# First phase by rows of four column blocks, norm factors by transposes, one small product block later

## The chip, the core and the metric

The kernel runs on one core of a Trainium2 chip. The metric is the device time of one execution in microseconds. The engines are TensorE (PE, matmuls; PEld is its weight load, which overlaps them), VectorE (DVE), ScalarE (ACT), GpSimd (POOL) and SyncE (SP, which issues most transfers).

## The reference

One layer of a hybrid decoder: 528 tokens (16 learned ones and 512 of x), 2048 features. The normalised input goes through one input projection, whose columns feed three causal mixers (gated DeltaNet with 6 heads, GLA with 5, forgetting attention with 5). Each branch has a SiLU gate, and one output projection with a residual and a last norm follows.

```python
h = rms_norm(x, norm_w)                       # x * rsqrt(mean(x*x) + eps) * norm_w
proj = (h @ w_in).astype(f32)                 # [528, 2048] @ [2048, IN_COLS]
(dq, dk, dv, dz, db, da, gq, gk, gv, gz, gl, fq, fk, fv, fz, ff) = split_cols(proj)
...
sol = lax.linalg.triangular_solve(eye + a_mat, rhs, ...)   # DeltaNet, chunks of 64
...
o_dn = gated_head_norm(o_dn, dz, dn_norm_w)
...
return x + o @ w_out                          # then rms_norm(., final_norm_w) over x's tokens
```

## The kernel before

x is held transposed: 16 tiles k of 128 features by 528 tokens. A projection block is 128 columns of `w_in`: its 16 weight tiles (128 x 128, one for each k) are multiplied with the 16 tiles of x and summed in PSUM. For accuracy each operand is split exactly into a high and a low part (`hi`, `lo` of a weight, `xh`, `xl` of x). ACT makes the high part by a cast, DVE the low part by a subtraction, and PE runs three products for each k: hi·xh, hi·xl, lo·xh. x is scaled by `norm_w` (one column of `cpk` for each k) in that split. The factor of each token, 1/rms, is applied later, when a block leaves PSUM: `rstd` holds it for all 128 partitions.

The first phase makes the four blocks `dz` 0 to 3 for the 512 tokens of x, without the learned ones, into four PSUM banks (`pp`). Its weights come by quarters: one transfer holds four k of one block, 128 x 512 numbers (`first_quarter`), so that a quarter of the phase has four transfers, casts and subtractions of weights (`w0q` to `w3q`), and four tiles of x. `load_x` splits x; `first_part` (L303) runs the products. x's tiles 0 and 1 come in a transfer each, the others in pairs. The scales come from `consts` in a transfer of their own that ACT issues (L122). Ten products of the tile `ones` stand ahead of the phase (L298), and one more behind its first matmul group (L324).

While the phase runs, ACT squares the tokens of `xtok` and `mtok` and sums them into `ssq`; `rsc` is 1/rms, one number for each token, tokens along partitions, five columns of 128. To bring it to all partitions, DVE makes five diagonal matrices `dg` (L347) and PE multiplies them with `ones` (L349) into `pr`; ACT copies it to `rstd`. The gate product (`pgate`, L420) is next on PE, then the block `dz` 4 and so on (L234). The gate values run through DVE and ACT into a scan (`gw`, L457), which PE transposes (`ptg`, L462) in the middle of block 4.

The triangular solve is a blockwise inverse (`dn_inverse`, for the heads' groups g = 0 and 1): inverses of 32 x 32 blocks on DVE, then products `pm` (L773) and `pl` (L782), 24 small ones each, with ACT copies between, then `pn` (L808). They are dropped into the row of projection matmuls by `behind(mm, n)`, which ties a product behind the n-th matmul of a projection counted from a mark.

A tile framework orders the instructions of each engine by a simulated timeline, within the ties that the code gives (`behind`, `paced`, priorities); each engine then runs its list in order. Tiles come from pools with a fixed number of buffers, and a transfer into a buffer waits until its former content was read: `raw` rows have 7 buffers, the pool `six` has 14, the token tiles `xt` share 6.

Of the kernel before, what the change touches and what calls it, by code (L numbers as in the profile page):

```python
# [8 lines left out]
F32 = mybir.dt.float32  # L9
F32R = mybir.dt.float32r  # L10
# [3 lines left out]
AF = mybir.ActivationFunctionType  # L14
ALU = mybir.AluOpType
# [3 lines left out]
P = 128  # L19
D = 2048  # L20
KT = D // P
NM = 16
S = 512
T = NM + S
# [7 lines left out]

DN_HEADS, GLA_HEADS, FOX_HEADS = 6, 5, 5
SH = 10
NK = 8
H1 = 1
SKIP = 1
# [40 lines left out]
GATE_COLS, COLS, BLOCK_OF = _cols()  # L78
# [1 line left out]


@with_exitstack
def tile_hybrid_trunk(ctx, tc, xT, xtok, mtok, w_gate, w_in, w_out, w_dn, consts, lmask, fin_w, out, dbg=None):
    nc = tc.nc
    ctx.enter_context(nc.allow_low_precision("operands are split exactly into two parts"))
    dbg = dbg or {}
# [4 lines left out]
    six = pool("six", 14)  # L91
# [8 lines left out]
    def t15(name, shape=(P, H, P), dt=F32):  # L100
        return wk.tile(list(shape), dt, tag="t15", bufs=6, name=name)

    V, A, G, PE = nc.vector, nc.scalar, nc.gpsimd, nc.tensor
# [7 lines left out]
    ident = cst.tile([P, P], F32, name="ident")  # L111
    make_identity(nc, ident)
    ones = t15("ones", (P, P))
# [6 lines left out]
    nwc, cwc = cpk[:, 0:16], cpk[:, 16:88].rearrange("p (b w) -> p b w", w=4)  # L120
# [50 lines left out]
    pace, splits, heads_, waits = [None, None], [], [], []  # L171
# [7 lines left out]
    def raw_rows(src, name):  # L179

        raw = row(f"raw{name}")[:, : src.shape[-1]]
        nc.sync.dma_start(out=raw, in_=src)
        return raw, name

    def split_rows(raw, name):

        n = raw.shape[-1]
        both = six.tile([P, 2, 512], F32R, tag="six", name=f"w{name}")
        hi, lo = both[:, 0, :n], both[:, 1, :n]
        split(raw, hi, lo)  # L190
        return hi, lo


    def part(name, n=512):
        return hp.tile([P, T], F32R, tag="x", name=name)[:, :n]
# [18 lines left out]
    def behind(mm, n):  # L214

        later.append((mm.ins, len(order) + n))
# [9 lines left out]
    xh, xl = [], []  # L226
# [29 lines left out]

    NF = 4

    def first_quarter(i, q):
        return raw_rows(w_in[BLOCK_OF["dz", i], q // 2][:, (q % 2) * 512 : (q % 2 + 1) * 512], f"{i}q{q}")

    xs = {}

    def fetch_x(c):
        xs[c] = six.tile([P, 2, T], F32, tag="six", name=f"xs{c}")
        if c > 0:
            nc.sync.dma_start(out=xs[c], in_=xT[:, 2 * c : 2 * c + 2, :])

    firsts = []

    def fetch_first():
        fetch_x(0)
        for j in range(2):
            nc.sync.dma_start(out=xs[0][:, j], in_=xT[:, j])
            firsts.append(first_quarter(j, 0))
        firsts.extend(first_quarter(i, 0) for i in (2, 3))
        fetch_x(1)

    def load_x(c):
        if c not in xs:
            fetch_x(c)
        t = xs[c]
        for j in range(2):
            k = 2 * c + j
            if c == 0 and j == 1:
                wq.append(split_rows(*firsts[0]))
            xh.append(part(f"xh{k}", T))
            xl.append(part(f"xl{k}", T))  # L290
            A.activation(xh[k], t[:, j], AF.Copy, scale=nwc[:, k : k + 1])
            V.scalar_tensor_tensor(out=xl[k], in0=t[:, j], scalar=nwc[:, k : k + 1],
                                   in1=xh[k].bitcast(F32), op0=ALU.mult, op1=ALU.subtract)


    pw = psm.tile([P, 512], F32, tag="m", name="warm")
    for i in range(10):
        PE.matmul(pw[:, :P], ones, ones, start=True, stop=True)  # L298

    def first_part(ps, q, hi, lo, j):  # L300
        k = 4 * q + j
        for wt, xx in ((hi, xh), (hi, xl), (lo, xh)):
            mm = PE.matmul(ps[:, :S], wt[:, j * P : (j + 1) * P], xx[k][:, NM:T],  # L303
                      start=(k == 0 and wt is hi and xx is xh), stop=(k == KT - 1 and wt is lo))
        return mm

    fetch_first()
    begun = [inproj_begin(("dz", h), False)[1:] for h in range(NF)]
    for q in range(4):
        wq = []  # L310
        load_x(2 * q)
        for i in range(NF):
            if q + i > 0:
                wq.append(split_rows(*(first_quarter(i, q) if q else firsts[i])))
            if i == 1 and q or i == NF - 1 and not q:
                load_x(2 * q + 1)
        for j in range(4):
            for i in range(NF):
                mm = first_part(begun[i][0][0], q, *wq[i], j)
                if q + j + i == 0:  # L320

                    with tc.issue_after(mm.ins):
                        for _ in range(1):
                            PE.matmul(pw[:, :P], ones, ones, start=True, stop=True)  # L324
        if q == 1:
            more_constants()
    for h in range(NF):
        done["dz", h] = [(p_[:, :n], t0, n) for p_, (t0, n) in zip(*begun[h])]
# [2 lines left out]
    rsc = wk.tile([P, 5], F32, tag="rsc", bufs=1, name="rsc")  # L331
# [10 lines left out]
    A.activation(rsc, rsc, AF.Exp, scale=-0.5)  # L342
    pr = [psm.tile([P, 512], F32, tag="m", name=f"pr{a}") for a in range(2)]
    for b in range(5):
        r = NM if b == 4 else P
        dg = t15(f"dg{b}", (P, P))
        V.tensor_scalar_mul(dg[:, :r], ident[:, :r], rsc[:, b : b + 1])  # L347
        o = pr[1][:, :NM] if b == 4 else pr[0][:, b * P : (b + 1) * P]
        PE.matmul(o, ones, dg[:, :r], start=True, stop=True)  # L349
    A.copy(rstd[:, NM:], pr[0])  # L350
    A.copy(rstd[:, :NM], pr[1][:, :NM])

# [275 lines left out]
    raw = {}  # L628
# [99 lines left out]
    def dn_inverse(g, st):  # L728
# [50 lines left out]
        for n in range(NN):  # L779
            for q in range(2):  # L780
                lo_, hi_ = slice(64 * q, 64 * q + 32), slice(64 * q + 32, 64 * q + 64)
                mm = PE.matmul(pl[lo_, n, :], xc[lo_, n, :], m1[lo_, n, :], start=True, stop=True)  # L782
                if g == 1 and n + q == 0:
                    behind(mm, PM[g] + 38)
        for q in range(2):
            A.copy(l1[64 * q : 64 * q + 32], pl[64 * q : 64 * q + 32])

# [843 lines left out]
def _layout(x, meta_tokens, norm_w, w_in, conv_w, a_log, dt_bias, dn_norm_w, w_gk2, b_gk,  # L1631
            gla_norm_w, b_f, w_out, final_norm_w):

    import numpy as np

    c = np.ascontiguousarray
    f = np.float32
    x, w_in, w_out = (np.asarray(a) for a in (x, w_in, w_out))
    xt = np.concatenate([np.asarray(meta_tokens), x[0]], 0).T.reshape(KT, P, T)
    wz = np.concatenate([w_in[0], np.zeros((D, 1), f)], 1)  # L1640
    wg = wz[:, np.asarray(GATE_COLS)].reshape(KT, P, 64).transpose(1, 0, 2).reshape(P, 1024)
    wz = wz[:, np.asarray(COLS)].reshape(2, 8, P, NBLK, P)
# [12 lines left out]
    lm = np.stack([(j // (2 * s) == i // (2 * s)) & (j // s % 2 == 0) & (i // s % 2 == 1)  # L1655
                   for s in (16, 8, 4, 2, 1)] + [j == i], 1).astype(np.int32)
    gk = np.zeros((P, 320), f)
    gk[:16] = gk[16:32] = gk[32:48] = np.asarray(w_gk2)[0]
    misc[:16, 7] = misc[16:32, 6] = misc[32:48, 7] = 1
    misc[16:32, 7] = -1  # L1660
    consts = np.concatenate([
        np.asarray(norm_w)[0].reshape(KT, P).T,
        np.asarray(conv_w)[0].reshape(4, 18, P).transpose(2, 1, 0).reshape(P, 72),
        misc, np.asarray(dn_norm_w)[0][:, None], np.asarray(gla_norm_w)[0][:, None],
        np.concatenate([np.asarray(b_gk)[0], np.zeros(64, f)]).reshape(3, P).T, gk], 1)
    return {
        "xT": c(xt.transpose(1, 0, 2)), "xtok": c(x[0]),
        "mtok": c(np.asarray(meta_tokens)),
        "w_gate": c(wg), "w_in": c(wz.transpose(3, 0, 2, 1, 4).reshape(NBLK, 2, P, 1024)),
        "w_out": c(wo.transpose(3, 0, 2, 1, 4).reshape(4, (16 - SH) // 2, P, 1024)),  # L1670
        "w_dn": c(wd.transpose(2, 0, 1, 3)),
        "consts": c(consts), "lmask": c(lm), "fin_w": c(np.asarray(final_norm_w)),
    }
# [15 lines left out]
```

## Time and profile before

| | |
|---|---|
| median of 3 runs | 974.25 us (973.39 to 974.83) |
| the profiled execution | 973.9 us, span 972.2 us |
| PE busy | 962.6 us, 99% |
| PEld busy | 887.4 us, 91% |
| DVE, ACT, POOL busy | 674.2, 476.7, 222.7 us |
| first phase, L303 | first matmul at 5.29 us, last at 50.71 us |
| small products `pl` of group 0 | 223.64 to 225.1 us |

Times in the profile are microseconds from the start of the span. A row of the timeline gives start, duration, engine, line, operation, output and inputs, the shapes, how many instructions it merges, and in brackets how long the engine was idle before it and what ended that. Matmuls are pipelined, so that their durations overlap; what one costs is the distance from its start to the next one's.

### The profile page before, as it was taken

To read this page: it belongs to the slowest core of one execution; us is meant where nothing else is said; L and a number is where in the kernel's file an instruction comes from. 1 tells how busy PE (TensorE), PEld (TensorE's weight loads), DVE (VectorE), ACT (ScalarE), POOL (GpSimd) and SP (SyncE) were. 2 spreads that over 40 slices of the span, in tenths; PEclk is the share of its full clock that TensorE was granted. 3 is DMA by queue.
4 is the path that set the end of the run, shared out by engine and by line. 5 is a ranking of instruction groups with operands and counts; after the bars stand their busy time and mean duration, and the time that the engine had idled before them with its cause. 6 is when DMAs were issued, how large, how long until landed. Compare 5 with 4: busy or idle time off the path is not lost.

```text
span 972.2 us, 18945 instructions
## 1 busy us (share of the span) xinstructions
PE 962.6 (99%) x7314; PEld 887.4 (91%) x7314; DVE 674.2 (69%) x1468; ACT 476.7 (49%) x1045; POOL 222.7 (23%) x243
## 2 busy tenths in 40 slices
PE   9999999999999999999999999999999999999996
PEld 7899999899999988899999989899999997888885
DVE  5468777877557986434695958866766768986664
ACT  6754533344456233434545545555555545654345
POOL 0033322232123225111213223222332120000023
PEclk9999999999999999999999999999999999999999
DMA  9835577987557797744647575577775588366534
GB/s 341 304 136 208 171 208 214 288 232 212 172 166 209 231 236 189 187 118 104 160 135 188 148 191 180 177 223 211 208 211 158 175 281 280 131 216 212 180 129 174
DMA packets 70335, 191.86 MB, mean 197 GB/s; under 512 B 14077, under 2 KB 17325, under 8 KB 69476
## 3 DMA queue, kind: packets, MB, share of 16 engines
q1 hardware_dynamic: 46048, 152.63, 44.7%
q0 software_dynamic: 15104, 31.66, 18.3%
q10 hardware_dynamic: 9092, 6.36, 2.4%
q8 instruction: 57, 0.93, 0.4%
q14 instruction: 34, 0.28, 0.1%
HBM read 179.93 MB, written 60.88 MB: 248 GB/s over the span
## 4 chain that ended last, share of the span: by engine, by line
PE 98%; DVE 1%; DMA 0%; issue 0%; ACT 0%; SPq 0%; DVEq 0%
PE pp L234 49%; PE pp_a L572 8%; PE pq L1413 6%; PE pp L303 5%; PE pa L1413 3%; PE pt L1413 3%; PE ps L1413 3%; PE pp_c L572 2%; PE pp_d L572 2%; PE pp_b L572 2%; PE pr L1413 1%; PE pss L1058 1%; PE pfo L1288 1%; PE pgate L420 1%; PE pfa L1240 1%; PE pg L716 1%
## 5 line engine op out<-in xcount | busy, mean ns | idle before, releaser
L234 PE MATMUL pp<-xh,wlo 128*128 128x264 f32 (+2 forms) x1120 | 269.8, 306 | 0.0
L234 PE MATMUL pp<-xl,whi 128*128 128x264 f32 (+2 forms) x1120 | 269.8, 305 | 0.0
L234 PE MATMUL pp<-xh,whi 128*128 128x264 f32 (+2 forms) x1120 | 269.7, 306 | 0.0
L166 ACT CAST whi<-raw 128x1024 fp32r<-128x1024 f32 x131 | 137.2, 1047 | 180.0 <-PE pp L234 120.6
L167 DVE TENSOR_TENSOR wlo<-raw,whi 128x1024 fp32r<-128x1024 f32 x131 | 161.0, 1229 | 56.8 <-ACT whi L166 44.4
L234 PEld LDWEIGHTS pp<-xh,whi 128*128 128x128 f32 x1120 | 181.5, 189 | 8.7 <-issue 0.2
L234 PEld LDWEIGHTS pp<-xh,wlo 128*128 128x128 f32 x1120 | 181.6, 189 | 8.5 <-issue 0.2
L234 PEld LDWEIGHTS pp<-xl,whi 128*128 128x128 f32 x1120 | 181.7, 189 | 8.2
L379 POOL TENSOR_SCALAR stc<-cv 128x528 f32<-128x528 f32 (+1 forms) x18 | 27.2, 1513 | 131.3 <-DVE cv L614 120.2
L614 DVE SCALAR_TENSOR_TENSOR cv<-pb,cpk,cv 128x528 f32<-128x528 f32 (+1 forms) x54 | 40.9, 757 | 0.9
L1442 POOL TENSOR_TENSOR acc<-acc,fw 128x512 f32<-128x512 f32 x4 | 6.1, 1544 | 138.7 <-DVE wll L167 138.7
L167 DVE TENSOR_TENSOR wlos<-raws,whis 128x1024 fp32r<-128x1024 f32 x20 | 24.3, 1224 | 14.9 <-ACT whis L166 14.7
L166 ACT CAST whis<-raws 128x1024 fp32r<-128x1024 f32 x20 | 20.7, 1048 | 27.3 <-PE pq L1413 10.3
L572 PE MATMUL pp_a<-t,whi 128*128 128x264 f32 (+1 forms) x224 | 29.5, 282 | 0.0
L572 PE MATMUL pp_a<-xl,whi 128*128 128x264 f32 x112 | 28.4, 288 | 0.0
L572 PE MATMUL pp_a<-xh,whi 128*128 128x264 f32 x112 | 28.1, 285 | 0.0
L486 POOL DMA_DIRECT2D tw<-tw x16 | 13.4, 840 | 62.8 <-DVE wlo L167 30.1
L368 DVE TENSOR_TENSOR pb<-pp,rstd 128x264 f32<-128x264 f32 (+1 forms) x36 | 13.8, 425 | 20.1 <-PE pp L234 20.0
L572 PEld LDWEIGHTS pp_a<-t,whi 128*128 128x128 f32 x224 | 27.7, 189 | 0.0
L379 POOL TENSOR_SCALAR stdz<-zdz 128x512 f32<-128x512 f32 x6 | 11.2, 1874 | 63.7 <-DVE zdz L397 55.3
L1413 PE MATMUL pq<-whia,a 128*128 128x512 f32 x80 | 25.5, 394 | 0.0
L1413 PE MATMUL pq<-whis,s 128*128 128x512 f32 x80 | 25.4, 394 | 0.0
(504 smaller groups left out, 2114.2 us busy)
## 6 DMA issues: line engine op xcount, KB each, us to landing
raw<-in_w_in SPq DMA_DIRECT2D x103, 512.0 KB, 4.0
ti<-in_w_in SPq DMA_DIRECT2D x28, 512.0 KB, 5.2
raw<-ti SPq DMA_DIRECT2D x28, 512.0 KB, 3.4
tw<-in_w_dn SPq DMA_DIRECT2D x20, 512.0 KB, 5.5
raws<-tw SPq DMA_DIRECT2D x15, 512.0 KB, 3.7
ti<-in_w_in POOLq DMA_DIRECT2D x14, 512.0 KB, 7.2
ti<-ti POOLq DMA_DIRECT2D x14, 512.0 KB, 7.5
tw<-in_w_dn POOLq DMA_DIRECT2D x10, 512.0 KB, 6.3
```

The source lines that it names most:

```text
L166: pace[0] = A.copy(hi, raw).ins
L167: pace[1] = V.tensor_tensor(out=lo, in0=raw, in1=hi.bitcast(F32), op=ALU.subtract).ins
L234: mm = PE.matmul(p_[:, :nt], wt[:, j * m : (j + 1) * m], xx[k][:, t0 : t0 + nt], start=(k == 0 and wt is hi and xx is xh), stop=(k == KT - ...
L303: mm = PE.matmul(ps[:, :S], wt[:, j * P : (j + 1) * P], xx[k][:, NM:T], start=(k == 0 and wt is hi and xx is xh), stop=(k == KT - 1 and wt ...
L368: V.tensor_tensor(out=o, in0=p_[rows], in1=rstd[rows, t0 : t0 + n], op=ALU.mult)
L379: maxes.append(G.tensor_scalar_max(t, src, LOW).ins)
L420: PE.matmul(pgate[a][:, :HT], wg[k // 8][:, k % 8, :], xx[k][:, a * HT : (a + 1) * HT], start=(k == 0 and xx is xh), stop=(k == KT - 1 and ...
L486: x = G.dma_start(out=out_[s], in_=in_[s], accum_op=ALU.add, max_dma_last_dim=2048)
L572: m = PE.matmul(p_[:, cols], wt[:, j * P : (j + 1) * P], xx[j][part_][:, cols], start=first and i == 0, stop=i == len(todo) - 1, skip_grou ...
L614: V.scalar_tensor_tensor(out=c, in0=pb[:, t0 + w : w + T], scalar=cwc[:, blk, w : w + 1], in1=c, op0=ALU.mult, op1=ALU.add)
L716: PE.matmul(pg[:r, j * r : (j + 1) * r], kT[:, j, ts], kT[:, j, ts], start=True, stop=True)
L1413: mm = PE.matmul(p_, o_[:, s], w_, start=(first and n == 0), stop=(last and n == 2), skip_group_check=True)
```

## The change

Three things.

The first phase goes by k instead of by quarters. For each k one transfer brings the 128 rows of weights of all four blocks (`w_first`, 128 x 512, laid out for it by the host), one cast and one subtraction split it, and PE runs hi·xh on the four blocks, then hi·xl, then lo·xh. For k = 0 the cast is in two halves of 256 columns. The scales come as 16 further columns of x's first tile (`x_first`) and serve k = 0 and 1; the others use `cpk` as before, whose transfer stays. Transfers are requested two pairs of x tiles ahead. Seven `ones` products stand ahead in place of ten, and the one inside the phase is gone.

The norm factors go to all partitions by five PE transposes of a column of `rsc`, repeated 128 times by its access pattern; the diagonals and their products are gone.

In `dn_inverse` the first product of `pl` of group 0 is tied behind a matmul too (mark `PM[0] + 26`); in group 1 it was already.

```diff
-    def first_quarter(i, q):
-        return raw_rows(w_in[BLOCK_OF["dz", i], q // 2][:, (q % 2) * 512 : (q % 2 + 1) * 512], f"{i}q{q}")
+    def fetch_w(k):
+        raws_first[k] = raw_rows(w_first[k], f"f{k}")
 
     def fetch_x(c):
+        if c == 0:
+            t = six.tile([P, 2, T + KT], F32, tag="six", name="xs0")
+            xs[0] = t[:, :, :T]
+            nc.sync.dma_start(out=t[:, 0], in_=x_first)
+            fetch_w(0)
+            nc.sync.dma_start(out=t[:, 1, :T], in_=xT[:, 1])
+            fetch_w(1)
+            return t[:, 0, T:]
         xs[c] = six.tile([P, 2, T], F32, tag="six", name=f"xs{c}")
...
+        nc.sync.dma_start(out=xs[c], in_=xT[:, 2 * c : 2 * c + 2, :])
+        fetch_w(2 * c)
+        fetch_w(2 * c + 1)
+
+    def load_x(k):
+        t, w = xs[k // 2][:, k % 2], (nwf if k < 2 else nwc)[:, k : k + 1]
+        xh.append(part(f"xh{k}", T))
+        xl.append(part(f"xl{k}", T))
+        x = A.activation(xh[k], t, AF.Copy, scale=w)
+        if k == 1:
+            paced(x)
+        if k == 0:
+            raw, name = raws_first[0]
+            both = six.tile([P, 2, 512], F32R, tag="six", name=f"w{name}")
+            hi, lo = both[:, 0], both[:, 1]
+            for c in (slice(0, 256), slice(256, 512)):
+                pace[0] = A.copy(hi[:, c], raw[:, c]).ins
+        V.scalar_tensor_tensor(out=xl[k], in0=t, scalar=w, in1=xh[k].bitcast(F32), op0=ALU.mult, op1=ALU.subtract)
+        if k > 0:
+            return split_rows(*raws_first[k])
+        pace[1] = V.tensor_tensor(out=lo, in0=raw, in1=hi.bitcast(F32), op=ALU.subtract).ins
...
-    for i in range(10):
+    for i in range(7):
         PE.matmul(pw[:, :P], ones, ones, start=True, stop=True)
...
+    nwf = fetch_x(0)
+    fetch_x(1)
+    for k in range(KT):
+        if k % 2 == 0 and k < KT - 4:
+            fetch_x(k // 2 + 2)
+        hi, lo = load_x(k)
+        for n, (wt, xx) in enumerate(((hi, xh), (hi, xl), (lo, xh))):
             for i in range(NF):
...
+                PE.matmul(begun[i][0][0][:, :S], wt[:, i * P : (i + 1) * P], xx[k][:, NM:T],
+                          start=k + n == 0, stop=k == KT - 1 and n == 2)
...
     for b in range(5):
-        r = NM if b == 4 else P
-        dg = t15(f"dg{b}", (P, P))
-        V.tensor_scalar_mul(dg[:, :r], ident[:, :r], rsc[:, b : b + 1])
-        o = pr[1][:, :NM] if b == 4 else pr[0][:, b * P : (b + 1) * P]
-        PE.matmul(o, ones, dg[:, :r], start=True, stop=True)
+        o = pr[b // 4][:, b % 4 * P : b % 4 * P + P]
+        PE.transpose(o, rsc[:, b : b + 1].to_broadcast([P, P]), ident)
...
-                if g == 1 and n + q == 0:
-                    behind(mm, PM[g] + 38)
+                if n + q == 0:
+                    behind(mm, PM[g] + (26, 38)[g])
```

PE's list at the start of the program, before (`pp0`, `pp1`, `pp2`, `pp12` are the four blocks, `w0q0` the first quarter of block 0):

```order
L298 MATMUL warm_99<-ones_84 128x128 x10
L303 MATMUL pp0_0_123<-xh0_127,w0q0_131 128x512
L303 MATMUL pp0_0_123<-xl0_128,w0q0_131 128x512
L303 MATMUL pp0_0_123<-xh0_127,w0q0_131 128x512
L324 MATMUL warm_99<-ones_84 128x128
L303 MATMUL pp0_0_123<-xh1_134,w0q0_131 128x512
L303 MATMUL pp1_0_124<-xh0_127,w1q0_138 128x512
L303 MATMUL pp1_0_124<-xl0_128,w1q0_138 128x512
L303 MATMUL pp0_0_123<-xl1_135,w0q0_131 128x512
L303 MATMUL pp0_0_123<-xh1_134,w0q0_131 128x512
L303 MATMUL pp2_0_125<-xh0_127,w2q0_141 128x512
```

The same place after the change (`wf0` and `wf1` are the weights of k = 0 and 1 for all four blocks):

```order
L303 MATMUL warm_99<-ones_84 128x128 x7
L314 MATMUL pp0_0_107<-xh0_130,wf0_133 128x512
L314 MATMUL pp1_0_108<-xh0_130,wf0_133 128x512
L314 MATMUL pp0_0_107<-xl0_131,wf0_133 128x512
L314 MATMUL pp1_0_108<-xl0_131,wf0_133 128x512
L314 MATMUL pp2_0_109<-xh0_130,wf0_133 128x512
L314 MATMUL pp12_0_110<-xh0_130,wf0_133 128x512
L314 MATMUL pp2_0_109<-xl0_131,wf0_133 128x512
L314 MATMUL pp12_0_110<-xl0_131,wf0_133 128x512
L314 MATMUL pp0_0_107<-xh0_130,wf0_133 128x512
...
L314 MATMUL pp0_0_107<-xh1_150,wf1_154 128x512
```

Before, the fourth matmul already needed x's second tile and the fifth a second block's weights; now twelve matmuls need only the weights and the tile of k = 0.

ACT's list at the same place, before:

```order
L291 ACTIVATE xh0_127<-xs0_110,cpk_90 128x528
L166 CAST w0q0_131<-raw0q0_112 128x512
L291 ACTIVATE xh1_134<-xs0_110,cpk_90 128x528
L166 CAST w1q0_138<-raw1q0_115 128x512
L166 CAST w2q0_141<-raw2q0_117 128x512
L166 CAST w3q0_144<-raw3q0_119 128x512
L291 ACTIVATE xh2_147<-xs1_121,cpk_90 128x528
```

And after:

```order
L283 ACTIVATE xh0_130<-xs0_111 128x528
L291 CAST wf0_133<-rawf0_113 128x256 x2
L283 ACTIVATE xh1_150<-xs0_111 128x528
L167 CAST wf1_154<-rawf1_116 128x512
L283 ACTIVATE xh2_175<-xs1_118,cpk_90 128x528
L167 CAST wf2_179<-rawf2_120 128x512
```

x's split no longer reads `cpk` for k = 0 and 1, and one weight cast stands between two tiles of x, where four casts came with the first two tiles.

PE's list around the product `pl` of group 0, in the middle of block `pp17`, before:

```order
L234 MATMUL pp17_0_2944<-xl7_231,whi17_0_2949 128x264
L782 MATMUL pl0_2166<-iv0_2129 32x32
L234 MATMUL pp17_1_2945<-xl7_231,whi17_0_2949 128x264
L782 MATMUL pl0_2166<-iv0_2129 32x32 x23
L234 MATMUL pp17_0_2944<-xh7_230,wlo17_0_2950 128x264
```

And after:

```order
L235 MATMUL pp17_0_2931<-xl7_283,whi17_0_2936 128x264
L235 MATMUL pp17_1_2932<-xl7_283,whi17_0_2936 128x264
L235 MATMUL pp17_0_2931<-xh7_282,wlo17_0_2937 128x264
L770 MATMUL pl0_2153<-iv0_2116 32x32 x24
L235 MATMUL pp17_1_2932<-xh7_282,wlo17_0_2937 128x264
```

The 24 products now stand together, two projection matmuls further back than the first of them stood. Elsewhere PE's list is as before, but for the transposes `ptg` (and `ptgm`), which stand one matmul further forward in block 4.

More of the change, by code (lines that the diff above doesn't have):

```diff
@@ L34 @@
 SH = 10
+NF = 4
 NK = 8
@@ L82, in tile_hybrid_trunk @@
 @with_exitstack
-def tile_hybrid_trunk(ctx, tc, xT, xtok, mtok, w_gate, w_in, w_out, w_dn, consts, lmask, fin_w, out, dbg=None):
+def tile_hybrid_trunk(ctx, tc, xT, x_first, w_first, xtok, mtok, w_gate, w_in, w_out, w_dn, consts, lmask, fin_w, out, dbg=None):
     nc = tc.nc
@@ L255, in inproj @@
         return done.pop(key)
-    NF = 4
-    def first_quarter(i, q):
-        return raw_rows(w_in[BLOCK_OF["dz", i], q // 2][:, (q % 2) * 512 : (q % 2 + 1) * 512], f"{i}q{q}")
-    xs = {}
+    xs, raws_first = {}, {}
+    def fetch_w(k):
+        raws_first[k] = raw_rows(w_first[k], f"f{k}")
     def fetch_x(c):
-        xs[c] = six.tile([P, 2, T], F32, tag="six", name=f"xs{c}")
[L268 to L293, printed above, removed]
+        if c == 0:
[6 more added lines that the diff above has]
+            return t[:, 0, T:]
@@ new lines, in fetch_x @@
+        xs[c] = six.tile([P, 2, T], F32, tag="six", name=f"xs{c}")
+        nc.sync.dma_start(out=xs[c], in_=xT[:, 2 * c : 2 * c + 2, :])
[18 more added lines that the diff above has]
+        pace[1] = V.tensor_tensor(out=lo, in0=raw, in1=hi.bitcast(F32), op=ALU.subtract).ins
+        splits.append(pace[1])
+        heads_.append(pace[0])
+        return hi, lo
@@ L296, in tile_hybrid_trunk @@
     pw = psm.tile([P, 512], F32, tag="m", name="warm")
-    for i in range(10):
+    for i in range(7):
         PE.matmul(pw[:, :P], ones, ones, start=True, stop=True)
[L300 to L307, printed above, removed]
@@ L308, in tile_hybrid_trunk @@
-    begun = [inproj_begin(("dz", h), False)[1:] for h in range(NF)]
[L309 to L317, printed above, removed]
-            for i in range(NF):
[L319 to L325, printed above, removed]
+    begun = [inproj_begin(("dz", h), False)[1:] for h in range(NF)]
@@ L326, in tile_hybrid_trunk @@
+    nwf = fetch_x(0)
[5 more added lines that the diff above has]
+        for n, (wt, xx) in enumerate(((hi, xh), (hi, xl), (lo, xh))):
+            for i in range(NF):
+                PE.matmul(begun[i][0][0][:, :S], wt[:, i * P : (i + 1) * P], xx[k][:, NM:T],
+                          start=k + n == 0, stop=k == KT - 1 and n == 2)
+        if k == 7:
             more_constants()
@@ L1666, in _layout @@
     return {
-        "xT": c(xt.transpose(1, 0, 2)), "xtok": c(x[0]),
+        "xT": c(xt.transpose(1, 0, 2)),
+        "x_first": c(np.concatenate([xt[0], np.asarray(norm_w)[0].reshape(KT, P).T], 1)),
+        "w_first": c(wz[:, :, :, [BLOCK_OF["dz", h] for h in range(NF)]].reshape(KT, P, NF * P)),
+        "xtok": c(x[0]),
         "mtok": c(np.asarray(meta_tokens)),
```

## The prediction

> **What bounds the kernel now.** I read the page's busy shares first, then the chain of waits, then TensorE's (PE's) timeline at the places that the change touches.
>
> ```profile
> PE 962.6 (99%) x7314; PEld 887.4 (91%) x7314; DVE 674.2 (69%) x1468; ACT 476.7 (49%) x1045; POOL 222.7 (23%) x243
> ```
> ```profile
> 2.17 4.45 DMA raw1q<-in_w_in
> 7.32 43.79 PE pp L303 x188
> ```
>
> PE is busy for 962.6 of 972.2 us, and from 7.32 us on the chain of the first phase is nothing but its own matmuls. So a term counts only if it changes how many microseconds of PE issue there are, or if it closes a hole in PE's work. The holes lie ahead of 7.65 us (start, duration, engine, line, operation):
>
> ```profile
> 1.19 4.34 PE L298 MATMUL warm<-ones 128*128 128x128 f32 x20 [1.19 <-POOL ones L114]
> 5.29 0.48 PE L303 MATMUL pp<-xh,w0q 128*128 128x512 f32 x1
> 5.61 0.43 PE L303 MATMUL pp<-xl,w0q 128*128 128x512 f32 x1
> 6.14 0.51 PE L303 MATMUL pp<-xh,w0q 128*128 128x512 f32 x1
> 6.48 0.39 PE L324 MATMUL warm<-ones 128*128 128x128 f32 x2
> 6.63 0.49 PE L303 MATMUL pp<-xh,w0q 128*128 128x512 f32 x1
> 7.32 0.50 PE L303 MATMUL pp<-xh,w1q 128*128 128x512 f32 x1 [0.20 <-ACT w1q L166]
> 7.65 0.39 PE L303 MATMUL pp<-xl,w1q 128*128 128x512 f32 x1
> ...
> 50.95 1.18 PE L349 MATMUL pr<-dg,ones 128*128 128x128 f32 x10
> 51.98 0.49 PE L420 MATMUL pgate<-xh,wg 128*128 128x264 f32 x2
> ```
>
> The phase has 192 matmuls of 512 columns. Five of them start before 7.65 us; the other 187 fill 7.65 to 50.95, which is 0.2315 us each, with no hole. The first five take 7.65 - 5.29 = 2.36 us where 5 x 0.2315 = 1.16 would do: 1.2 us are lost because four column blocks are wanted and only one of them has arrived.
>
> **The start, term 1.** What the first matmuls wait for, on ScalarE (ACT) and VectorE (DVE), and the two transfers ahead of them (KB each, us from issue to landing):
>
> ```profile
> 3.95 0.73 ACT L291 ACTIVATE xh<-xs,cpk 128x528 fp32r<-128x528 f32 x1 [1.88 <-DMA cpk<-in_consts]
> 4.59 0.60 ACT L166 CAST w0q<-raw0q 128x512 fp32r<-128x512 f32 x1
> 4.72 0.77 DVE L292 SCALAR_TENSOR_TENSOR xl<-xs,cpk,xh 128x528 fp32r<-128x528 f32 x1 [4.72 <-ACT xh L291]
> 5.82 0.74 ACT L291 ACTIVATE xh<-xs,cpk 128x528 fp32r<-128x528 f32 x1 [0.63 <-DMA xs<-in_xT]
> 6.64 0.62 ACT L166 CAST w1q<-raw1q 128x512 fp32r<-128x512 f32 x1
> 8.48 0.62 ACT L166 CAST w3q<-raw3q 128x512 fp32r<-128x512 f32 x1 [0.55 <-DMA raw3q<-in_w_in]
> ```
> ```profile
> xs<-in_xT SPq DMA_DIRECT2D x2, 264.0 KB, 2.9
> raw0q<-in_w_in SPq DMA_DIRECT2D x1, 256.0 KB, 3.2
> ```
>
> Step by step. x's first transfer is issued at 0.80 and lands 2.9 us later, at 3.7; xh waited to 3.95 for the scales (cpk), which now ride in that transfer (272 KB for 264). So xh runs 3.75 to 4.48. The first weights, issued at 1.24, land at 4.4; before, their cast took 0.60 us and PE began 0.1 us after it. Now the cast is in two halves. A half of 256 columns costs between 0.30 us (half of 0.60) and 0.60; I take 0.40. First half: 4.43 to 4.83; first matmul: 4.93. It serves blocks 0 and 1, and the third matmul needs xl: DVE starts it at 4.52, 0.77 us, done at 5.29, 0.12 us to PE as before (5.49 to 5.61): 5.41, after two matmuls 5.40. The second half of the cast ends near 5.2, for the fifth matmul at 5.88; the low part (DVE, estimated at 0.7 us from the cast's 0.60 over the same columns, begun at xl's end) is there at 6.0, for the ninth at 6.8. Twelve matmuls now hang on one 256 KB block, where before three did.
>
> Row 1 of x still arrives at 5.8 and weights 1 at 6.62 (2.17 + 4.45): xh 5.84 to 6.58, cast 6.66 to 7.28, on PE at 7.4; wanted at 5.41 + 10 x 0.2315 = 7.73. Margin 0.3 us. Row 2 needs x rows 2 and 3 in one 528 KB transfer and weights 2: 1.6 MB stand ahead of x's landing, as many as ahead of raw3q, which landed at 8.46; weights 2 then take some 0.7 us more, cast by 9.8; wanted at 10.5. From there PE takes a pair of rows (0.53 MB) in 12 x 0.2315 = 2.78 us, so the margin grows. The same 25 loads of x and weights go through SyncE's queue; the token loads x of `xtok` now stand further back in it, which matters only for `rsc`, below.
>
> Phase end: 5.41 + 190 x 0.2315 = 49.40 instead of 50.95. **Term 1: -1.55 us.** Bounds: with a full 0.60 us cast -1.35; if the halving costs 0.30 nothing more is won, since xl sets the third matmul: -1.55. The loss of an earlier clock, below, has its own case. The filler product at 6.48 that goes away stood in a hole and is worth nothing.
>
> **Norm factors, term 2.** Ten PE records (five products in two passes) fill 50.95 to 51.98: 1.03 us. The trace has transposes of the same shape against the same identity, one pass each:
>
> ```profile
> 74.28 0.60 PE L462 MATMUL ptg<-ident,gw 128*128 128x128 f32 x4
> 74.71 0.27 PE L464 MATMUL ptgm<-ident,gw 128*16 128x128 f32 x1
> ```
>
> Four start within 74.71 - 74.28 = 0.43, 0.108 us each; five are 0.54. **Term 2: -0.49 us.** What is new is that the loaded operand is one column repeated. If that loads like two passes it is ten records again: 0 to +0.07. I take the transposes' row, since a load of 128 columns is in both. The five diagonals on DVE that go stood between this row and PE's products, which came 6.9 us later:
>
> ```profile
> 43.87 0.21 ACT L342 ACTIVATE rsc<-rsc 128x5 f32<-128x5 f32 x1
> ```
>
> `rsc` is there at 44.1; PE now wants it at 49.4. The square sums behind it may come up to 5 us later before PE would stand; the same bytes pass the same queue, so I charge nothing.
>
> **The inverse product, term 3.** The block of 24 small products (48 records) in one piece, and now in the piece-and-rest form that the change joins:
>
> ```profile
> 219.43 0.28 PE L234 MATMUL pp<-xl,whi 128*128 128x264 f32 x1
> 219.64 0.95 PE L773 MATMUL pm<-iv,an 32*32 32x32 f32 x48
> 220.51 0.39 PE L234 MATMUL pp<-xl,whi 128*128 128x264 f32 x1
> 220.75 0.41 PE L234 MATMUL pp<-xh,wlo 128*128 128x264 f32 x2
> 220.99 0.29 PE L234 MATMUL pp<-xh,whi 128*128 128x264 f32 x1
> ...
> 223.43 0.28 PE L234 MATMUL pp<-xl,whi 128*128 128x264 f32 x1
> 223.64 0.24 PE L782 MATMUL pl<-iv 32*32 32x32 f32 x2
> 223.82 0.39 PE L234 MATMUL pp<-xl,whi 128*128 128x264 f32 x1
> 224.14 0.94 PE L782 MATMUL pl<-iv 32*32 32x32 f32 x46
> 225.01 0.51 PE L234 MATMUL pp<-xh,wlo 128*128 128x264 f32 x2
> 225.36 0.40 PE L234 MATMUL pp<-xh,whi 128*128 128x264 f32 x2
> ```
>
> A matmul of 264 columns takes (220.99 - 220.75) / 2 = 0.12. In one piece: 220.75 - 219.43 less two of them = 1.08 us. Split: 225.36 - 223.43 less four = 1.45. Each trip to the small tiles and back costs about 0.37 beside its work, and one trip goes. **Term 3: -0.37 us**; lower bound of the gain 0, if the new neighbours part it again. Its results come 0.12 us later; their last reader ahead of PE is this copy, and PE takes it 3.7 us after its end:
>
> ```profile
> 227.89 0.35 DVE L796 COPY uf<-iv 32x384 f32<-32x384 f32 x1
> 231.94 0.45 PE L808 MATMUL pn<-uf,an 64*64 64x64 f32 x8
> ```
>
> Sum: -1.55 - 0.49 - 0.37 = **-2.41 us**. The profiled execution took 973.9 us (span 972.2, 1.7 around it): 971.5. The median shown, 974.25, lies 0.35 above it: **971.9**, 0.25% faster.
>
> **The rivals.** (1) The clock. Twenty warm records in 4.34 us are 0.217 each, but the ten at 50.95 took 0.10 to 0.11: PE runs at half speed at first, and the step comes near 5.0 us, 3.8 us after its first matmul. The granted clock at the other end (us of the stretch, busy us of the five engines, granted clock, DMA):
>
> ```profile
> 964.00:967.00 3.00, 0.54 (x5) 0.33 (x3) 2.08 (x8) 2.02 (x6) 0.00 (x0) 1.00 0.89 311
> 967.00:968.00 1.00, 0.00 (x0) 0.00 (x0) 0.25 (x1) 0.36 (x1) 0.00 (x0) 0.83 0.85 318
> ```
>
> 0.83 is two thirds of that microsecond at full and the rest at half speed: the clock falls at about 967.66, 3.1 us after PE's last matmul (964.54). So something looks at 3 to 4 us of PE's past. Seven warm products end at 1.19 + 14 x 0.217 = 4.2; PE then stands 0.7 us, which the ten of before covered. If a stretch with that hole does not count, the step comes about 3.8 us after 4.93, at 8.7, and half speed costs (8.7 - 4.93) / 2 = 1.9 us: 973.8, no change. For it: nothing in this trace shows a stretch with a hole that counted. Against: the hole is a fifth of the stretch.
> The Trainium skill ("TensorE: Matmul & The Clock Gate", section "What's actually happening") says that full clock comes after one busy window of about 3.4 us, and that the window runs free of the kernel's start. The 3.8 and 3.1 us above agree with such a length; by the strict reading, a fully busy window, the step would fall between 8.3 and 11.8 us and the time between 973.6 and 975.3. No row here shows how busy is busy enough.
>
> (2) Slower than before: the same gate, where the short holes of row 0 and row 1 (the xl wait at 5.4, the 0.3 us margin at 7.4) spoil the next stretch too. The step is then at 4.93 + 2 x 3.8 = 12.5, the price 3.8 us, the time 975.7. It decides once the step comes later than 4.93 + 2 x 2.41 = 9.75 us.
>
> (3) A new wait behind the first phase. PE reaches the gate transposes (74.28) 2.0 us sooner. Their input is this scan, ready at 73.10:
>
> ```profile
> L457 DVE TENSOR_TENSOR_SCAN gw<-gw x1: 1246/1246/1246, 71.9 to 71.9; 17x528 f32<-17x528 f32 x1
> ```
>
> Slack is 1.18 us. If the scan did not move, PE would stand 2.04 + 0.12 - 1.18 = 1.0 us: 972.9. Against: the scan's chain starts from the norm factors and the gate product, which PE itself makes sooner. A late second row (margins 0.3 and 0.7 us) would cost about as much.
>
> (4) The change does not do what it says: the transposes take two passes and the small block is parted again: only term 1, 972.7.
>
> **How the numbers follow.** Forecast 0.60, rival 1 0.18, rival 2 0.07, rivals 3 and 4 together 0.15. A measurement of this kernel can tell about 0.2%, 1.95 us, so faster means below 972.3. The forecast's own range is 971.2 to 972.7, four fifths of it below 972.3: 0.48, and a third of rivals 3 and 4: faster 0.53. Rival 2 with the clock later still, or two rivals at once, passes 976.2: slower 0.06. The rest, 0.41, is no change. The range 970.9 to 974.0 holds the forecast and rivals 1, 3 and 4 and leaves out rival 2 and a tail below.
>
> **What would show it.** Right: first matmul near 4.9, no hole of PE between 5.4 and 49.5, `pr` in about 0.55 us, one `pl` block of 48 records, and the gate transposes near 72.2 without a wait. Wrong: matmuls of 512 columns 0.43 us apart beyond 6 us (the clock), PE waiting for xh or weights of row 1 or 2, ten `pr` records, or a wait at `ptg`.

## The result, and the profile after

The changed kernel takes 972.29 us (median of 22 runs, 970.94 to 975.21); the kernel before took 974.36 us beside it (22 runs, 973.39 to 976.83). The ratio is 0.9979, 95% interval 0.9974 to 0.9985: 0.21% faster, 2.07 us, where 2.41 us and 971.9 us were forecast. The profiled execution took 972.28 us, with a span of 970.6 us against 972.2 before.

The first line of the page of the kernel after, with the busy time of each engine, and everything that PE waited for (microseconds in total, times, longest):

```profile
PE 960.8 (99%) x7301; PEld 885.2 (91%) x7301; DVE 673.0 (69%) x1463; ACT 476.4 (49%) x1046; POOL 221.2 (23%) x243
```
```profile
PE warm L303 <- POOL ones L115: 1.2, 1, 1.2
PE pp L314 <- ACT wf L291: 0.3, 1, 0.3
PE pfx L1246 <- DVE fm L1241: 0.2, 1, 0.2
```

PE is busy for 1.8 us less. It waits once for the first weights, and the gate transposes (`ptg`) are not in the list. The timeline of the start (start, duration, engine, line, operation):

```profile
3.65 0.73 ACT L283 ACTIVATE xh<-xs 128x528 fp32r<-128x528 f32 x1 [1.57 <-DMA xs<-in_x_first]
4.42 0.71 ACT L291 CAST wf<-rawf 128x256 fp32r<-128x256 f32 x2
4.41 0.77 DVE L292 SCALAR_TENSOR_TENSOR xl<-xs,xh 128x528 fp32r<-128x528 f32 x1 [4.41 <-ACT xh L283]
1.19 3.35 PE L303 MATMUL warm<-ones 128*128 128x128 f32 x14 [1.19 <-POOL ones L115]
4.87 1.17 PE L314 MATMUL pp<-xh,wf 128*128 128x512 f32 x2 [0.33 <-ACT wf L291]
5.88 0.62 PE L314 MATMUL pp<-xl,wf 128*128 128x512 f32 x2
6.34 0.62 PE L314 MATMUL pp<-xh,wf 128*128 128x512 f32 x2
```

`xh` starts as x lands and the half casts follow. The first two matmuls take 5.88 - 4.87 = 1.01 us, the next two 6.34 - 5.88 = 0.46: PE ran at half speed until about 5.86. The other places of the change, in the same view (the scan is DVE's):

```profile
48.95 1.10 PE L314 MATMUL pp<-xh,wf 128*128 128x512 f32 x4
49.89 0.71 PE L337 MATMUL pr<-ident,rsc 128*128 128x128 f32 x5
50.35 0.49 PE L408 MATMUL pgate<-xh,wg 128*128 128x264 f32 x2
69.40 1.25 DVE L445 TENSOR_TENSOR_SCAN gw<-gw 17x528 f32<-17x528 f32 x1
72.53 0.60 PE L450 MATMUL ptg<-ident,gw 128*128 128x128 f32 x4
222.32 0.29 PE L235 MATMUL pp<-xh,wlo 128*128 128x264 f32 x1
222.54 0.95 PE L770 MATMUL pl<-iv 32*32 32x32 f32 x48
223.42 0.39 PE L235 MATMUL pp<-xh,wlo 128*128 128x264 f32 x1
223.64 0.40 PE L235 MATMUL pp<-xh,whi 128*128 128x264 f32 x2
```

Phase end 49.89 (50.95 before), five `pr` records in 50.35 - 49.89 = 0.46 us (ten in 1.03 before), `pl` in one block. PE's last matmul ends at 962.63, 1.9 us sooner than before.

### The profile page after: what moved, and what is told of

It is laid out like the page before. It is cut to its first block, busy times and chain, and to the rows that moved or that the text cites. A ratio compares the mean times of both kernels' runs of the same rounds, so it can differ in the third digit from the quotient of the medians.

```text
span 970.6 us, 18917 instructions
## 1 busy us (share of the span) xinstructions
PE 960.8 (99%) x7301; PEld 885.2 (91%) x7301; DVE 673.0 (69%) x1463; ACT 476.4 (49%) x1046; POOL 221.2 (23%) x243
## 4 chain that ended last, share of the span: by engine, by line
PE 98%; DVE 1%; issue 0%; DMA 0%; ACT 0%; SPq 0%; DVEq 0%
PE pp L235 49%; PE pp_a L560 8%; PE pq L1401 6%; PE pp L314 5%; PE pa L1401 3%; PE pt L1401 3%; PE ps L1401 3%; PE pp_c L560 2%; PE pp_d L560 2%; PE pp_b L560 2%; PE pr L1401 1%; PE pss L1046 1%; PE pfo L1276 1%; PE pgate L408 1%; PE pfa L1228 1%; PE pg L704 1%
## 5 line engine op out<-in xcount | busy, mean ns | idle before, releaser
L314 PE MATMUL pp<-xh,wf 128*128 128x512 f32 x128 | 33.1, 398 | 0.3 <-ACT wf L291 0.3
L314 PEld LDWEIGHTS pp<-xh,wf 128*128 128x128 f32 x128 | 24.2, 190 | 6.1 <-ACT wf L291 0.6
```

Of the source, the lines that this page charges most:

```text
L314: PE.matmul(begun[i][0][0][:, :S], wt[:, i * P : (i + 1) * P], xx[k][:, NM:T], start=k + n == 0, stop=k == KT - 1 and n == 2)
```

## Experiments

Each ratio is to the kernel before, with its 95% interval; the medians of the kernel before were 973.9 to 974.0 us in these runs.

**The parts by themselves.** Is the whole the sum of its parts, or does a later place hand some of it back? One kernel has only the new first phase, one only the other two edits.

```diff
# phase_alone: the kernel after, with the old factors and the old tie
-        PE.transpose(o, rsc[:, b : b + 1].to_broadcast([P, P]), ident)
+        V.tensor_scalar_mul(dg[:, :r], ident[:, :r], rsc[:, b : b + 1])
+        PE.matmul(o, ones, dg[:, :r], start=True, stop=True)
-                if n + q == 0:
-                    behind(mm, PM[g] + (26, 38)[g])
+                if g == 1 and n + q == 0:
+                    behind(mm, PM[g] + 38)
# rest_alone: the kernel before, with the reverse of these lines
```

> The first phase by rows of four blocks alone; norm factors and the inverse product as before. Theory (terms add up, clock as in the changed kernel's trace): first matmul near 4.9 us, phase end between 49.4 us (clock at full speed by then) and 50.0 us, so 1.0 to 1.5 us less than before, ratio 0.9985 to 0.9990. Rival (the phase gains nothing of its own, the gain is in the other two parts): ratio 1.000.

> Kernel before with the transposes and the joined inverse product, first phase as before. Theory: the factors take 0.46 us of PE instead of 1.03 and the joined block 1.08 instead of 1.45, together -0.9 us, ratio 0.9990, and together with the phase alone the whole change of about -2.05. Rival (a late wait gives part of an early lead back): the two parts add up to more than the whole change, by about 0.3 us.

Measured: the phase alone 972.92 us, ratio 0.9989 (0.9980 to 0.9997); the rest alone 973.13 us, 0.9990 (0.9981 to 0.9998). The timeline of the phase alone:

```profile
4.78 0.73 PE L314 MATMUL pp<-xh,wf 128*128 128x512 f32 x2 [0.23 <-ACT wf L291]
5.35 0.63 PE L314 MATMUL pp<-xl,wf 128*128 128x512 f32 x2
49.34 1.18 PE L340 MATMUL pr<-dg,ones 128*128 128x128 f32 x10
```

and of the rest alone:

```profile
50.91 0.71 PE L346 MATMUL pr<-ident,rsc 128*128 128x128 f32 x5
51.38 0.49 PE L417 MATMUL pgate<-xh,wg 128*128 128x264 f32 x2
```

With full speed from its first matmul the new phase ends at 49.34, 1.61 us sooner. The rest takes `pr` from 1.03 to 0.47 us. The gains, 1.05 and 0.84 us of the medians, add up to 1.9, which is the whole within the intervals; each is known to about 0.8 us, so a loss of some tenths between them would not show. The phase's profiled execution (972.09 us) is one of its fastest: its median gain, 1.05, is smaller than the profile's 1.61.

**The products ahead.** Ten leave no hole before the first matmul; one leaves PE idle for most of the start.

```diff
-    for i in range(7):
+    for i in range(10):      # warm10
+    for i in range(1):       # warm1
         PE.matmul(pw[:, :P], ones, ones, start=True, stop=True)
```

> Changed kernel with ten products ahead of the phase instead of seven, so that PE has no hole before its first matmul. Theory (a stretch of 3.4 us counts as busy above a share between 37% and 84%): the clock steps up in the same range as with seven; ten slow products would end near 5.4 us and can push the first matmul from 4.9 to 5.4; time the same to +0.5 us. Rival (a stretch must be busy throughout): with seven the step came late in most executions, and ten are faster by 1 us or more.

> Changed kernel with one product ahead of the phase instead of seven: PE is idle until its first matmul at 4.9 us. Theory (share between 37% and 84% of a 3.4 us stretch): the clock steps up between 6.1 and 11.2 us, the first phase ends 0.1 to 2.7 us later than with seven, about 1.2 us in the middle; matmuls of 512 columns stand 0.43 us apart until the step. Rival (the clock needs no products ahead, or data is late anyway): phase end unchanged within 0.3 us.

Measured: ten 971.94 us, 0.9979 (0.9970 to 0.9988); one 973.91 us, 1.0000 (0.9991 to 1.0008). With one the first matmul starts no later, but:

```profile
4.80 1.22 PE L314 MATMUL pp<-xh,wf 128*128 128x512 f32 x2 [2.81 <-ACT wf L291]
5.82 1.05 PE L314 MATMUL pp<-xl,wf 128*128 128x512 f32 x2
6.67 1.05 PE L314 MATMUL pp<-xh,wf 128*128 128x512 f32 x2
7.53 0.88 PE L314 MATMUL pp<-xl,wf 128*128 128x512 f32 x2
8.24 2.00 PE L314 MATMUL pp<-xh,wf 128*128 128x512 f32 x8
```

Pairs are 0.85 apart up to 7.5 and 0.46 from 8.24 on; the clock rose near 8.06. (8.06 - 4.80) / 2 = 1.6 us are lost at half speed, 1.1 more than in the kernel after, whose `pgate` comes 1.0 us sooner. By the ratios the whole gain is gone (0.9979 and 1.0000, 2.0 us apart), so the products are worth 1.0 us in these two profiles and about 2 us in the medians. With ten the first matmul starts at 5.48, 0.6 us later, and nothing is lost that can be measured: the clock rose at 5.92, and most of what PE does before that moment is done at half speed. A gain of 1 us or more, which the rival in that run's expectation asked for, is not there.

**Does an early lead arrive at the end?** In after's profile PE leads the kernel before by about 1.75 us at 225 to 350 us, by 1.39 at 362 and by 1.9 at the end. Around 350 PE's weight load stood for a low part that DVE made late, behind work of the second inverse, whose input `ab` had landed at 336.6 us:

```profile
349.22 0.19 PEld L235 LDWEIGHTS pp<-xh,wlo 128*128 128x128 f32 x1 [0.29 <-DVE wlo L168]
360.54 0.19 PEld L235 LDWEIGHTS pp<-xh,wlo 128*128 128x128 f32 x1 [0.40 <-DVE wlo L168]
```

Theory A: this place is a cap that takes back what comes early. Theory B: a lead goes through whole. Sixteen matmuls (3.7 us) are left out of the first phase, or the same number after that place; and three weight loads of 512 KB that run beside the inverse's input are held back, with and without the shorter phase.

```diff
 # less_early, in the first phase
+            if n == 1 and k >= 12:
+                continue
 # less_late, in the output projection (mms): 16 products of hi by the low part
+            if less and n == 1:
+                continue
 # held: SP's prefetches 42 to 44 are moved to later turns
-        if moves:
+        count[0] += 1
+        if moves and count[0] not in (42, 43, 44):
 # held_less: both less_early and held
```

> Changed kernel without the product hi*xl for k = 12 to 15 of the first phase: 16 matmuls, 3.7 us of PE less, ahead of everything. Theory A (the lead is cut near 330 to 362 us, where VectorE's inverse of group 1 starts at the landing of a transfer that does not move with PE, and PE then waits for weight parts behind it): most of the 3.7 us is gone after 362 us, time within 0.8 us of the changed kernel, 971.5 to 972.5. Theory B (what PE saves early arrives whole): 968.6.

> Changed kernel without the product of the high part of the operand with the low part of the weights for 16 matmuls of 512 columns in the output projection (second of four column groups, first two pairs of weight tiles), late in the program: also 3.7 us of PE. Control: by A and by B alike about 968.6, 3.7 us less than the changed kernel; if it is less, PE's time is not what bounds the end either.

> Changed kernel with three prefetch transfers (512 KB each, of w_dn into tw) held back from 312 to 335 us to later loads; no engine's list of work changes. Theory A with the transfers' queue as cause: the inverse's input (ab from scr) lands about 1 us sooner than at 336.6, VectorE starts the inverse then, PE has no hole at 349 and 360 us: 0.3 us less than the changed kernel. Rival (the landing hangs on the many small pieces of that transfer, not on its neighbours): landing and holes unchanged.

> Both: the 16 early matmuls left out (the product hi*xl for k = 12 to 15 of the first phase) and the three transfers held. Theory A with the queue as cause: 1 us or more of the 3.7 us that are lost without the holding come through, time about 1 us under the run with the products left out alone. Rival (landing not moved by its neighbours): same time as that run. Theory B: 968.6 or less.

| kernel | median us | ratio | `ab` landed | PE's end, profile |
|---|---|---|---|---|
| after | 972.29 | 0.9979 (0.9974 to 0.9985) | 336.64 | 962.63 |
| less_early | 968.84 | 0.9951 (0.9937 to 0.9964) | 330.11 | 958.29 |
| held | 971.86 | 0.9985 (0.9976 to 0.9994) | 333.08 | 961.58 |
| held_less | 968.71 | 0.9953 (0.9939 to 0.9966) | 329.17 | 958.46 |
| less_late | 974.54 | 1.0007 (0.9997 to 1.0017) | | |

Theory A falls. Of 3.7 us left out early, 3.15 arrive between the medians of held and held_less, which ran on the same chip, and 3.45 between after and less_early (4 runs each of less_early and held_less); PE's end moves by 3.1 and 4.3 us. Nor does the transfer of `ab` stand still, as A assumed: in less_early it was issued at 326.34 (330.56 in after) and landed at 330.11 (336.64). Holding the loads back gives nothing that can be told (held_less stands 0.1 us from less_early, where A expected about 1). The stalls at 349 and 360 are one execution's: the same kernel taken once more (below) has none.

less_late is no control, as it was meant to be: products are tied behind the n-th matmul of a projection, so leaving matmuls out moves others (`pfw` starts at 829.0 in after, at 843.6 here), and it is 2.3 us slower than after. Its profile shows a new wait, and what it does to the clock (PE's longest wait, then us of the stretch, busy us of PE, PEld, DVE, ACT and POOL, granted clock, DMA):

```profile
PE pfw L1268 <- DVE fm L1241: 2.3, 1, 2.3
```
```profile
841.28:844.69 3.41, 1.16 (x6) 0.93 (x6) 3.41 (x11) 2.19 (x6) 0.00 (x0) 1.00 0.48 154
844.69:848.10 3.41, 3.41 (x9) 2.38 (x8) 3.41 (x5) 0.39 (x2) 0.00 (x0) 0.50 0.44 144
```

PE stands 2.25 us at 841 to 843.6, and the whole next stretch of 3.41 us runs at half speed though PE is busy in all of it. Half of 3.41 is 1.7: the wait cost 2.25 us and 1.7 us more. Three further waits that after does not have (0.6, 0.5 and 0.3 us) make it 5.3 us in all, against the 3.7 us left out.

**Is PE what ends the program?** The same sixteen matmuls left out of the last blocks.

```diff
 # less_last, in the output projection, last pair of k, first two column blocks
+            if less and n == 1:
+                continue
```

> Changed kernel without the product of the operand's high part with the weights' low part for 16 matmuls of 512 columns in the last stage (two of the four column groups of the last pair of weight tiles), 3.7 us of PE, where no product of another branch is tied to a count of projection matmuls any more. Theory (what PE saves arrives where nothing else is late; the earlier run with 16 matmuls less in the output projection was slower because products tied to the count met VectorE's last softmax chain): 3.0 to 3.7 us less than the changed kernel. Rival (the last 170 us are bound by the weights' arrival or the sums on VectorE, not by PE): 1 us less or nothing.

Measured: 972.83 us, 0.9992 (0.9983 to 1.0002); not faster than after. The last stage of after and then of less_last (us of the stretch, busy us of PE, PEld, DVE, ACT and POOL, granted clock, DMA share, GB/s):

```profile
955.00:960.00 5.00, 5.00 (x31) 4.40 (x30) 2.96 (x7) 3.64 (x9) 0.11 (x1) 1.00 0.88 299
960.00:965.00 5.00, 2.63 (x23) 2.42 (x21) 3.89 (x13) 3.43 (x10) 0.00 (x0) 1.00 0.89 305
965.00:971.00 6.00, 0.00 (x0) 0.00 (x0) 0.34 (x1) 0.45 (x1) 0.00 (x0) 0.50 0.55 198
```
```profile
955.00:960.00 5.00, 4.38 (x36) 4.13 (x34) 4.82 (x14) 4.34 (x15) 1.79 (x2) 1.00 0.57 196
960.00:965.00 5.00, 0.00 (x0) 0.00 (x0) 2.57 (x6) 3.13 (x7) 0.00 (x0) 0.92 1.05 379
965.00:971.00 6.00, 0.00 (x0) 0.00 (x0) 0.00 (x0) 0.00 (x0) 0.00 (x0) 0.50 0.62 223
```

PE ends 3.25 us sooner, DVE and ACT are done before 965, and the span is 970.9 for 970.6. Both move the same 4.2 MB of output in these 16 us (299 x 5 + 305 x 5 + 198 x 6 KB); in less_last the first of it leaves later (196 for 299 GB/s to 960) and 379 GB/s follow. So PE's time alone does not set the end, though the chain of waits in after runs over PE's matmuls up to 962.64. That the output transfers set it, with the sums and scaling that feed them, is read from these rows and was not tried by itself. A rival stays: the edit also moved the sums, for the first output transfer is issued at 956.22 in less_last and at 954.97 in after, and an edit that left this order alone might have gained. Matmuls left out of the first phase were worth their time; these sixteen were worth nothing.

**Three single executions.** After unaltered; the first scales taken from `cpk` again; the first cast in one piece.

```diff
 # scale_apart
-(nwf if k < 2 else nwc)[:, k : k + 1]
+nwc[:, k : k + 1]
 # whole_cast
-for c in (slice(0, 256), slice(256, 512)):
+for c in (slice(0, 512),):
```

> The changed kernel unaltered, a second profile. Theory (the two holes of PE at 349 and 360 us in its first profile, 0.35 us, came from a late landing of the inverse's input in that one execution, 336.6 us against 333.1 to 335.2 in other kernels with the same lists): landing before 336 us and no hole there; first matmul again at 4.8 to 4.9 us, the clock's step between 4.6 and 5.9 us. Rival (the holes belong to the changed kernel): the same holes.

> Changed kernel, but the scales of k = 0 and 1 read from the separate transfer of cpk, as before the change. Theory: x's first split waits for that transfer and starts at 3.9 to 4.0 us instead of 3.65, the first matmul comes at 5.1 to 5.2 instead of 4.87: 0.15 to 0.3 us. Rival (the first weights' landing at 4.39 sets the start): first matmul still at 4.9.

> Changed kernel, but the first weights' cast in one piece. Theory: the cast takes 0.6 us from 4.4, first matmul at 5.1 instead of 4.87, 0.2 us; the low part's products come later in the list and wait for nothing. Rival (the low part of x sets the third matmul anyway): phase end unchanged within 0.1 us where the clock steps at the same time.

After, once more: 972.11 us. Its first matmul is at 4.86, but the clock rose a microsecond later than in the first profile, beyond what was expected:

```profile
4.86 1.22 PE L314 MATMUL pp<-xh,wf 128*128 128x512 f32 x2 [0.31 <-ACT wf L291]
5.88 1.05 PE L314 MATMUL pp<-xl,wf 128*128 128x512 f32 x2
6.73 0.70 PE L314 MATMUL pp<-xh,wf 128*128 128x512 f32 x2
```

Its `pgate` is 0.5 us later than in the first profile, and its span is 970.4 us all the same, without the stalls at 349 and 360. DVE begins on `ab` at 335.60, for 336.76 in the first.

Scales apart: 975.77 us, slower than the kernel before's median of 974.0.

```profile
3.98 0.73 ACT L283 ACTIVATE xh<-xs,cpk 128x528 fp32r<-128x528 f32 x1 [1.91 <-DMA cpk<-in_consts]
5.06 1.22 PE L314 MATMUL pp<-xh,wf 128*128 128x512 f32 x2 [0.52 <-ACT wf L291]
...
7.79 1.06 PE L314 MATMUL pp<-xl,wf 128*128 128x512 f32 x2
8.64 2.53 PE L314 MATMUL pp<-xh,wf 128*128 128x512 f32 x8
...
52.25 0.49 PE L408 MATMUL pgate<-xh,wg 128*128 128x264 f32 x2
```

The expected part came: the first matmul 0.19 us later. The unexpected part is larger: pairs stay 0.85 us apart until 9.75, and `pgate` is 1.9 us later than in after. Half speed costs (9.75 - 5.06) / 2 = 2.3 us here, 0.5 in after. This is what rival 1 described. That the longer hole before the first matmul (0.52 us for 0.33) brought it fits the stretches in the last section, but it is one execution. The span is 3.5 us longer than after's; the larger part of the other 1.6 us came much later, where PE waited 1.2 us for `fm` of DVE (0.2 in after), so that not all of 975.77 is the clock's.

One cast: 973.64 us. x landed a little sooner in this execution:

```profile
4.30 0.62 ACT L291 CAST wf<-rawf 128x512 fp32r<-128x512 f32 x1
4.97 1.20 PE L314 MATMUL pp<-xh,wf 128*128 128x512 f32 x4 [0.46 <-ACT wf L291]
...
49.54 0.71 PE L337 MATMUL pr<-ident,rsc 128*128 128x128 f32 x5
50.01 0.49 PE L408 MATMUL pgate<-xh,wg 128*128 128x264 f32 x2
```

Its first matmul is 0.1 us later than after's, and its phase still ends sooner (`pgate` 50.01 for 50.35), because the clock was at full speed from 4.33. The list now had four hi·xh products ahead of hi·xl, so nothing waited for `xl`. The kernel to compare with is the phase alone, which has the two half casts (the first from 4.33, for 4.30 here) and also ran its first matmul at full speed: first matmul 4.78 there and 4.97 here, phase end 49.34 and 49.54. So halving the cast gained the 0.2 us that were expected, by one execution of each. The 1.3 us more in the span came later, in waits for DVE of 0.9 and 0.8 us; their cause was not looked for.

## Why the prediction was right, and where it was not

**The sum.** Forecast -2.41, measured -2.07 (median), -1.6 (span of the profiled executions). That the kernel is faster stands outside the noise. That its median, 972.29, came out below the prediction's line for "faster", 972.3, is chance.

**Term 1, the start (-1.55).** Right at full clock: the phase alone ended at 49.34, 49.40 was forecast. Short in the kernel after, 49.89 (-1.06): the mis-sized step is "phase end: 5.41 + 190 x 0.2315", which took every matmul at full speed. In after the clock rose at 5.86, and (5.86 - 4.87) / 2 = 0.50 us went to half speed, which is the whole difference. This loss is not fixed: it was nothing in the phase alone and (6.86 - 4.86) / 2 = 1.0 us in after's second execution, so a sum at full speed takes the best case. The first matmul came at 4.87 (forecast 4.93), the half cast took 0.40 (taken 0.40). Rows 1 and 2 caused no wait, as forecast.

**Term 2, the norm factors (-0.49).** Five single-pass records in 0.46 us, so -0.57: the transposes of the repeated column cost 0.09 each where 0.108 was taken. The bound "loads like two passes" did not come true.

**Term 3, the joined inverse product (-0.37).** (223.64 - 222.32) less two matmuls of 0.12 is 1.08 us, 1.45 before: -0.37, as forecast.

The three as measured, -1.06 - 0.57 - 0.37 = -2.0, come near PE's lead at its end (1.9) and the median's gain, but in part by chance. Right behind the third edit the lead is 225.36 - 223.64 = 1.7 us: some 0.3 us went between 51 and 222 us, for a cause not looked for. The stalls at 349 and 360 took another 0.35, and 0.5 came back later, 0.2 of it where PE waited 0.2 us for `fm` of DVE instead of 0.4; no term names these.

**Rival 1, the clock.** Wrong for this kernel, right as a mechanism. Of the ten profiles with seven products, seven have the whole hole before the first matmul in a stretch that counted; in whole_cast and the phase alone the stretch ended at 4.33 and 4.62, before the hole or just in it. In scale_apart the stretch with the hole did not count, and half speed cost 2.3 us, where the working named 1.9. The change may stand near an edge, for an operand 0.2 us later was enough in that one execution. Whether after's slowest runs (973.9 and 975.2 us) are such executions stays open, as no profile caught one. **Rival 2**, two spoiled stretches, did not occur. **Rival 3**, a wait at the gate transposes: wrong. The scan ended at 69.40 + 1.25 = 70.65, 2.5 us sooner than before (73.1), as the argument against that rival said, its chain starts from PE's own work; the slack grew from 1.18 to 1.9 us. **Rival 4** is refuted by the five `pr` records and the block of 48.

One assumption went unsaid: that a microsecond of PE is worth a microsecond anywhere. It held for these terms, all before 225 us (less_early); the one edit tried in the last stage gained nothing (less_last).

## What to carry to other kernels

At the start, count the work that PE does before its first useful matmul together with the holes in it: in one execution here an operand 0.2 us later went with a clock that rose 3.9 us later, at a price of about 2 us. Price an edit of PE's work by the stage that it is in: sixteen early matmuls were worth their time here, sixteen of the last stage nothing. An experiment that leaves work out can move the work tied to it; look at its order and waits before reading its time.

## What the runs showed of the hardware

The clock step was not expected to be this regular. At the start of each profile the matmul spacing changes at one instant, from 0.43 to 0.23 us, and the clock falls again after the end: in after at 965.0 (granted clock 1.00 to 965 and 0.50 from there, above). From 5.86 to 965.0 are 959.1 us, and less_late's half-speed stretch was 3.41 us long; 281 such stretches of 3.413 us are 959.1. In the kernel before the fall at 967.66 and the step at 5.09 lie 962.6 apart, 282 of them. So the chip seems to look at PE in stretches of 3.413 us, and where their borders lie differs from run to run: in kernels with seven products the step came between 4.33 and 6.86, and at 9.75 in scale_apart.

How busy a stretch must be shows in the stretches that ended at a border. First those that the clock followed with full speed (before, after, and less_late's start, the least busy of all; columns as in the last stage):

```profile
1.68:5.09 3.41, 3.41 (x18) 3.41 (x18) 0.37 (x1) 1.53 (x3) 0.55 (x6) 1.00 0.93 264
```
```profile
2.45:5.86 3.41, 3.08 (x12) 2.63 (x12) 1.44 (x2) 1.51 (x4) 0.00 (x0) 1.00 1.00 348
```
```profile
1.59:5.00 3.41, 3.05 (x15) 2.76 (x14) 0.41 (x1) 1.66 (x4) 0.65 (x6) 1.00 0.93 280
```

and then two that it did not follow (the second execution of after, whose step came a stretch later, and scale_apart):

```profile
0.04:3.45 3.41, 2.25 (x10) 2.26 (x11) 0.00 (x0) 1.28 (x1) 1.60 (x15) 1.00 0.46 130
```
```profile
2.93:6.34 3.41, 2.90 (x11) 2.42 (x11) 1.59 (x3) 1.97 (x4) 0.00 (x0) 1.00 1.03 345
```

(The granted clock column reads 1.00 there, where the spacing of the matmuls shows half speed; the spacing is what was used.) With 3.05 of 3.41 us busy (89%) and more, PE got full speed in all fourteen profiles; with 2.90 (85%) and less it did not, and less_late's 1.16 (34%) took the clock away inside the program. If busy time is what is looked at, the bound for gaining full speed lies between 2.90 and 3.05 us, on the word of one profile at either side. Keeping it takes less. This stretch of scale_apart, between two borders and far inside the program, left the clock at 1.00, in the next stretch too:

```profile
651.46:654.87 3.41, 2.20 (x18) 1.94 (x17) 3.41 (x6) 1.35 (x5) 1.69 (x3) 1.00 0.96 267
```

So full speed was kept with 2.20 us (64%) and lost with 1.16. The expectation of the run with ten products put the bound for gaining it between 37% and 84%; scale_apart's 85%, which the clock did not follow, puts it higher. The Trainium skill ("TensorE: Matmul & The Clock Gate", section "What's actually happening") tells of one busy window of about 3.4 us that runs free of the kernel's start: the length and the free running agree with the 3.413 us here. Its strict reading in the prediction, a fully busy window, does not: 89% were enough.

After's seven products end at 1.19 + 3.35 = 4.54 by its profile, 0.33 us before the first matmul. An eighth (0.43 us at half speed) would fill that hole, and by this reading the first stretch with work in all of it would count; it was not tried.
